# A decoder trunk: norms after the output projection, an own key buffer, attention levels issued together, outputs by ScalarE

## The chip, the cores and the metric

The kernel runs on one core of a Trainium2 chip. The metric is the device time of one execution in microseconds. The engines are named as in the profile: PE is TensorE (matrix products and transposes), PEld its loading of weights, DVE is VectorE, ACT is ScalarE, POOL is GpSimd, and SP issues the transfers. Each engine takes its instructions in the order in which they were placed in its queue, and waits on semaphores for results of others.

## What is computed

Two layers over 16 meta tokens and 2048 tokens of width 1024, all in fp32. The first is a gated convolution module, the second gated linear attention (GLA) with 4 heads, keys of 128 and values of 256. Each layer ends with `h = LayerNorm(alpha * h + mixer(h))`. Cut to what matters here:

```python
def conformer_mixer(h, ...):
    a, ga, z = split(h @ w_in + b_in, 3)
    c = causal_depthwise_conv31(a * sigmoid(ga)) + b_dw
    c = silu(layer_norm(c, norm_g, norm_b))
    return (c * silu(z)) @ w_out + b_out

def gla_mixer(h, ...):
    q, k, v, r, a1 = split(h @ w_in)
    g = log_sigmoid(a1 @ w_a2 + b_a) / 16
    # per chunk and head, b = cumsum(g) in the chunk:
    o = (q * exp(b)) @ S + att @ v,   att[t, s] = sum_d q[t,d] k[s,d] exp(b[t,d] - b[s,d]),  s <= t
    S = exp(b_last) * S + (k * exp(b_last - b)).T @ v
    o = o * rsqrt(mean(o * o) + eps) * norm_g
    return (o * silu(r)) @ w_out
```

## The kernel before, in words

Every large product is made three times: an fp32 operand is split into a high and a low part of a faster format (`split`, L72 to L74: ScalarE copies the high part, another engine subtracts), and `mm3` (L102 to L108) adds hi x hi, hi x lo and lo x hi into one PSUM tile. A scheduler orders the instructions of each engine when the program is built; the code's order is its input and buffer counts are its bounds. The order on TensorE is then fixed.

There are four stages. The first (to about 590 us) makes the convolution's inputs and taps, and isn't touched. The second (about 555 to 775 us) goes over 17 tiles of 128 tokens (`SUBS`; the last has 16): `norm(i)` (L311 to L337) loads the convolution's outputs into one of four buffers c, makes the mean by a small product (`mean`, L323), squares on ScalarE, adds up on GpSimd (`tree`), makes the variance by a small product (L330), a power on GpSimd, a diagonal dg (L334), a product `rb` (L335) that spreads the scale over the partitions, and multiplies c by it (L336). `gate(i)` (L345 to L357) does eight silus on ScalarE (L351), multiplies by silu(z) (L354), and splits the result into h_gt (ScalarE) and l_gt (VectorE). `out_proj(i)` (L418 to L425) makes the 48 products of 512 columns `y{i}`, adds the residual and does the layer norm. The loop (L427 to L435) runs norm, gate, projection; a head start before it has done three norms and one gate. A tile's y can't start before its h_gt.

The third stage (about 780 to 1550 us) is GLA: four blocks of 512 tokens (the first with the 16 meta tokens more) by four heads, so 16 units. `proj_units` issues the projections of the next head (k, q, v, r, and in `gates`, L626 to L643, the decay's cumulative sum b), and `gla_units` (L651 to L801) the work of the unit, in pieces that are interleaved by a debt counter in `phase3`. A unit does: kh = k exp(b_last - b) (L682 to L685: GpSimd, ScalarE, VectorE), its transposes pk (L693), the state products ds and the running state S (`state`), and the attention matrix of a 128-token chunk in levels m = 64, 32, 16, 8, 4, 2. For each level GpSimd (L719, L720), ScalarE and VectorE (L722, L723) make the decayed q and k, the tile A; levels 64 to 16 go into the PSUM tile att by products on sub-tiles of the array (L729), the rest into sm (L758, L760), which VectorE masks and reduces to red (32 by 32 blocks). at = red on the diagonal blocks plus att is split to a_h, a_l; the outputs o (L106 to L108) are squared on ScalarE with a sum (L783), copied (L784), scaled by the root mean square (L786 to L789), transposed (oT) and gated. The meta tokens' key buffer khm (L658) shares the tag kh and its one buffer with kh; kh's tile is also the place into which Square writes.

The last stage (about 1535 to 1727 us) is the output projection of GLA with its layer norm, and isn't touched.

Of the kernel before, what the change touches and what calls it, by code (L numbers as in the profile page):

```python
# [11 lines left out]
F32 = mybir.dt.float32  # L12
F32R = mybir.dt.float32r
AF = mybir.ActivationFunctionType
ALU = mybir.AluOpType
# [4 lines left out]
P = 128  # L20
# [15 lines left out]
RMS_EPS = 1e-6  # L36
# [13 lines left out]
class Trunk:  # L50
# [349 lines left out]
    def phase2(self, x_tok, wo, rows, h1_d, tail):  # L400
        nc = self.nc
# [10 lines left out]
        for i in range(3):  # L412
            t = const.tile([P, D], F32, name=f"row{i}")
# [14 lines left out]
        for i in range(ns):  # L428
            self.norm_next()
            self.gate_next()  # L430
            if self.nnorm == ns and not self.normed and self.st2:
                self.st2.close()
                self.st2 = None
                tail()
            out_proj(*self.gated.popleft())  # L435
        left.close()

# [19 lines left out]
    def phase3_init(self, wa2, pp, og_d):  # L457
        nc = self.nc
        self.og_d = og_d
        c0 = self.pool(self.st3, name="p3a", bufs=1)  # L460
# [4 lines left out]
        c = self.pool(self.st3, name="p3c", bufs=1)  # L465
        self.prm = c.tile([P, 8], F32, name="prm3")
        nc.sync.dma_start(self.prm[:, 0:6], pp)
        nc.vector.tensor_scalar(self.prm[:, 6:8], self.prm[:, 4:6], 0.5, None, op0=ALU.mult)

        raw = self.raw("a2")[:, :512]  # L470
# [155 lines left out]
    def gates(self, bi, h, hd, ns):  # L626
# [4 lines left out]
        for c0, m in ns:  # L631
            ps = self.pjt(f"z{bi}_{h}_{c0}")[:, :m]
            nc.tensor.matmul(ps, lhsT=self.wa2[:, h * P : (h + 1) * P], rhs=self.ah[:, c0 : c0 + m], start=True, stop=True)
            nc.vector.tensor_scalar(gl[:, c0 : c0 + m], ps, ba, 0.0, op0=ALU.add, op1=ALU.min)
            nc.scalar.activation(b[:, c0 : c0 + m], ps, AF.Abs, bias=ba)
        nc.scalar.activation(b[:, :n], b[:, :n], AF.Exp, scale=-1.0)
        nc.scalar.activation(b[:, :n], b[:, :n], AF.Ln, bias=1.0)
        nc.vector.tensor_tensor(gl[:, :n], gl[:, :n], b[:, :n], op=ALU.subtract)
        o = n - 512
# [11 lines left out]
    def gla_units(self, h, hd, bi, t0, n):  # L651
# [4 lines left out]
        if off:  # L656

            kh = self.gp.tile([P, 512], F32, tag="kh", name=f"khm{h}", bufs=1)[:, :off]  # L658
            nc.gpsimd.tensor_tensor(kh, b[:, off - 1 : off].to_broadcast([P, off]), b[:, :off], op=ALU.subtract)
# [32 lines left out]
        for c in range(4):  # L692
            nc.tensor.transpose(pt[:, c], kh4[:, c], K.ident)  # L693
        kth, ktl = self.pair3("k", pt, nc.vector, nm)
        Ss = []
# [17 lines left out]
        for m in (64, 32, 16, 8, 4, 2):  # L713
            A = self.gp.tile([P, 512], F32, tag="A", name=f"A{nm}_{m}", bufs=4)
            view = lambda x: x.rearrange("p (s u i) -> p s u i", u=2, i=m)
# [9 lines left out]
            if m >= 16:  # L725
                for c in range(4):
                    for s in range(0, P, 2 * m):
                        a = c * P + s
                        nc.tensor.matmul(  # L729
                            att[s : s + m, c, s + m : s + 2 * m],  # L730
                            lhsT=A[:, a : a + m],
                            rhs=A[:, a + m : a + 2 * m],
                            start=False,
                            stop=False,
                            skip_group_check=True,
                        )
                state(len(Ss))
                yield

# [10 lines left out]
        for c2 in range(2):  # L750
# [11 lines left out]
            nc.vector.tensor_tensor(ms, sm, K.lmask.unsqueeze(1).to_broadcast([P, 2, 144]), op=ALU.mult)  # L762
            rd = red[:, 2 * c2 : 2 * c2 + 2]
            nc.vector.tensor_reduce(rd, ms[:, :, 16:].rearrange("p c (l t) -> p c t l", t=32), axis=mybir.AxisListType.X, op=ALU.add)
            odd = rd.rearrange("p c (s u) -> p c s u", u=2)[:, :, :, 1]
            nc.vector.tensor_tensor(odd, odd, ms[:, :, :16], op=ALU.add)
            yield
        at = self.gp.tile([P, 4, 4, 32], F32, tag="at", name=f"at{nm}", bufs=1)
        for c in range(4):
            nc.vector.tensor_tensor(at[:, c], red[:, c].unsqueeze(1).to_broadcast([P, 4, 32]), K.blk, op=ALU.mult)  # L770
        nc.vector.tensor_tensor(at, at, att.rearrange("p c (a b) -> p c a b", b=32), op=ALU.add)
        ath, atl = self.pair3("a", at.rearrange("p c a b -> p c (a b)"), nc.gpsimd, nm, 1)
# [4 lines left out]
        junk = kh[:, :256]  # L777
        for c2 in range(2):
            o2 = self.pt.tile([P, 2, 256], F32, tag="g", name=f"o{nm}_{c2}")
            for c in (2 * c2, 2 * c2 + 1):  # L780
                o = o2[:, c % 2]
                self.mm3(o, [(qh[:, c], ql[:, c], *Ss[c]), (ath[:, c], atl[:, c], vh[:, c], vl[:, c])])
                nc.scalar.activation(junk, o, AF.Square, accum_out=sq[:, 0, c : c + 1])  # L783
            nc.vector.tensor_copy(osb[:, 2 * c2 : 2 * c2 + 2], o2)  # L784
            yield
        nc.vector.tensor_scalar(sq[:, 1], sq[:, 0], 1.0 / 256, RMS_EPS, op0=ALU.mult, op1=ALU.add)  # L786
        nc.gpsimd.tensor_tensor(sq[:, 2], sq[:, 1], self.mhalf, op=ALU.pow)
        for c in range(4):
            nc.vector.tensor_scalar(osb[:, c], osb[:, c], sq[:, 2, c : c + 1], None, op0=ALU.mult)  # L789
        yield  # L790
# [167 lines left out]
```

## Time and profile before

| | us |
|---|---|
| median of three runs (lowest, highest) | 1737.01 (1736.24, 1739.46) |
| the profiled execution | 1736.39 |
| its span in the trace | 1734.4 |
| PE busy in the span | 1679.1 (97%) |
| PEld busy | 1491.7 (86%) |
| DVE busy | 1396.5 (81%) |
| ACT busy | 841.4 (49%) |
| POOL busy | 938.4 (54%) |

The profile is that of one execution. Busy times are summed over instructions; a pipelined product counts as busy from its start to its modelled end, so what tells TensorE's rate is the distance of one start from the next. A wait is idle time of an engine, put down to the instruction that released it.

### The profile page before, as it was taken

What the parts mean: (1) busy time and instruction counts of PE and PEld (TensorE: products, weight loads), DVE (VectorE), ACT (ScalarE), POOL (GpSimd) and SP (SyncE); (2) the same over time, 40 slices, a digit from 0 to 9 for tenths busy, and PEclk for the clock granted to TensorE, in tenths of its full rate; (3) what the DMA queues carried; (4) which work ended last, traced back from release to release, by engine and by line L of the source; (5) the groups of instructions that cost most, each with busy time, mean ns of one, the idle gap of its engine ahead of it and who ended that gap; (6) DMA issues with size and microseconds to landing.
All of it is one profiled execution on the core that took longest, in us unless ns stands there. A gap on an engine that the chain in (4) does not pass through costs nothing.

```text
span 1734.4 us, 29031 instructions
## 1 busy us (share of the span) xinstructions
PE 1679.1 (97%) x11715; PEld 1491.7 (86%) x11715; DVE 1396.5 (81%) x1869; ACT 841.4 (49%) x1269; POOL 938.4 (54%) x675
## 2 busy tenths in 40 slices
PE   8999999999998998999999999999999999999998
PEld 8999999999998776778888888888888888788886
DVE  5789999999998898877776787777887788787665
ACT  6445555655544544445545454555555465541000
POOL 1879999999985788766332243332443153331000
PEclk9999999999999999999999999999999999999999
DMA  7110111111146644443122322223223322355441
GB/s 247 37 37 37 37 69 42 74 52 59 72 146 206 207 148 142 142 139 106 50 86 87 111 84 88 74 87 111 78 75 106 123 74 84 126 170 169 147 134 61
DMA packets 103910, 178.72 MB, mean 103 GB/s; under 512 B 8624, under 2 KB 68400, under 8 KB 103776
## 3 DMA queue, kind: packets, MB, share of 16 engines
q1 hardware_dynamic: 103776, 176.86, 30.4%
q8 instruction: 92, 1.51, 0.4%
q14 instruction: 42, 0.34, 0.1%
HBM read 134.70 MB, written 42.14 MB: 102 GB/s over the span
## 4 chain that ended last, share of the span: by engine, by line
PE 69%; DVE 12%; POOL 8%; ACT 5%; issue 3%; DMA 3%; SPq 0%; DVEq 0%; POOLq 0%; ACTq 0%
PE pj_y L106 4%; PE pj_y L108 4%; PE pj_y L107 4%; PE pj_g L107 3%; PE pj_g L108 3%; PE pj_g L106 3%; PE pj_z L107 3%; PE pj_z L106 3%; PE pj_a L107 3%; PE pj_a L106 3%; PE pj_z L108 3%; PE pj_a L108 3%; POOL A L720 1%; POOL A L719 1%; PE att L729 1%
## 5 line engine op out<-in xcount | busy, mean ns | idle before, releaser
L196 POOL TENSOR_TENSOR gacc<-gacc,prod 128x1024 f32<-128x1024 f32 (+1 forms) x156 | 385.9, 2477 | 63.1 <-ACT prod L195 54.2
L204 DVE SCALAR_TENSOR_TENSOR cacc<-glu,prm,cacc 128x1024 f32<-128x1024 f32 (+1 forms) x292 | 374.8, 1294 | 7.0
L195 ACT ACTIVATE prod<-glu,prm 128x1024 f32<-128x1024 f32 (+1 forms) x156 | 179.1, 1155 | 107.7 <-POOL gacc L196 107.3
L719 POOL TENSOR_TENSOR A<-b 128x256 f32<-128x256 f32 x96 | 80.2, 836 | 269.9 <-PE att L729 105.6
L106 PE MATMUL pj_g<-xh,h_w 128*128 128x412 f32 (+1 forms) x320 | 113.7, 355 | 5.6 <-ACT h_w L73 4.2
L107 PE MATMUL pj_g<-xl,h_w 128*128 128x412 f32 (+1 forms) x320 | 113.5, 355 | 0.3 <-DVE xl L74 0.3
L108 PE MATMUL pj_y<-woh,l_gt 128*128 128x512 f32 (+1 forms) x272 | 109.0, 406 | 4.3 <-DVE l_gt L74 4.2
L106 PE MATMUL pj_y<-woh,h_gt 128*128 128x512 f32 (+1 forms) x272 | 110.7, 410 | 1.9 <-ACT h_gt L73 1.8
L108 PE MATMUL pj_g<-xh,l_w 128*128 128x412 f32 (+1 forms) x320 | 112.5, 353 | 0.0
L107 PE MATMUL pj_z<-xl,h_w 128*128 128x412 f32 (+1 forms) x320 | 112.3, 351 | 0.0
L106 PE MATMUL pj_z<-xh,h_w 128*128 128x412 f32 (+1 forms) x320 | 112.2, 351 | 0.0
L107 PE MATMUL pj_a<-xl,h_w 128*128 128x412 f32 (+1 forms) x320 | 112.2, 351 | 0.0
L106 PE MATMUL pj_a<-xh,h_w 128*128 128x412 f32 (+1 forms) x320 | 112.1, 350 | 0.0
L108 PE MATMUL pj_z<-xh,l_w 128*128 128x412 f32 (+1 forms) x320 | 112.0, 351 | 0.0
L108 PE MATMUL pj_a<-xh,l_w 128*128 128x412 f32 (+1 forms) x320 | 111.9, 350 | 0.0
L107 PE MATMUL pj_y<-wol,h_gt 128*128 128x512 f32 (+1 forms) x272 | 110.6, 406 | 0.0
L106 PE MATMUL pj_y<-w4h,h_g 128*128 128x512 f32 x256 | 99.9, 391 | 0.0
L107 PE MATMUL pj_y<-w4l,h_g 128*128 128x512 f32 x256 | 99.8, 390 | 0.0
L108 PE MATMUL pj_y<-w4h,l_g 128*128 128x512 f32 x256 | 99.7, 389 | 0.0
L388 POOL TENSOR_TENSOR rs<-rs,mhalf 128x1 f32<-128x1 f32 x16 | 14.8, 923 | 155.7 <-DVE rs L387 155.7
L377 DVE SCALAR_TENSOR_TENSOR xt<-xt,pj_y 128x512 f32<-128x512 f32 (+1 forms) x66 | 44.5, 677 | 59.2 <-PE pj_y L108 59.2
L654 ACT ACTIVATE A<-A 128x512 f32<-128x512 f32 (+1 forms) x112 | 66.3, 597 | 46.0 <-POOL A L720 43.1
(428 smaller groups left out, 5264.0 us busy)
## 6 DMA issues: line engine op xcount, KB each, us to landing
r_w<-w SPq DMA_DIRECT2D x24, 512.0 KB, 3.2
c<-c_d SPq DMA_DIRECT2D x16, 512.0 KB, 4.5
szb<-sz_d SPq DMA_DIRECT2D x16, 512.0 KB, 4.6
xt<-x_tok SPq DMA_DIRECT2D x16, 512.0 KB, 4.5
h_d<-xt SPq DMA_DIRECT2D x16, 512.0 KB, 2.7
r_h1b<-h_d SPq DMA_DIRECT2D x16, 512.0 KB, 3.6
og_d<-og SPq DMA_DIRECT2D x32, 256.0 KB, 3.9
xt<-h_d SPq DMA_DIRECT2D x16, 512.0 KB, 3.5
```

Source lines behind the costliest of these rows:

```text
L106: mm(out, lhsT=lh, rhs=rh, start=(i == 0), stop=False)
L107: mm(out, lhsT=lh, rhs=rl, start=False, stop=False)
L108: mm(out, lhsT=ll, rhs=rh, start=False, stop=(i == n - 1))
L195: nc.scalar.activation(pr, src(k), AF.Copy, scale=tap(k))
L196: nc.gpsimd.tensor_tensor(st["g"], st["g"], pr, op=ALU.add)
L204: nc.vector.scalar_tensor_tensor(out, src(k), tap(k), acc, op0=ALU.mult, op1=ALU.add)
L377: self.nc.vector.scalar_tensor_tensor(xt[:m, es], xt[:m, es], ALPHA, ps, op0=ALU.mult, op1=ALU.add)
L388: nc.gpsimd.tensor_tensor(rs[:n, 2:3], rs[:n, 1:2], self.mhalf[:n, 0:1], op=ALU.pow)
L654: ex = lambda o, i: nc.scalar.activation(o, i, AF.Exp, scale=1.0 / TAU)
L719: nc.gpsimd.tensor_tensor(Av[:, :, 0], mid, bv[:, :, 0], op=ALU.subtract)
L720: nc.gpsimd.tensor_tensor(Av[:, :, 1], bv[:, :, 1], mid, op=ALU.subtract)
L729: nc.tensor.matmul(att[s : s + m, c, s + m : s + 2 * m], lhsT=A[:, a : a + m], rhs=A[:, a + m : a + 2 * m], start=False, stop=False, skip_ ...
```

## The change

1. The loop of the second stage calls `norm_next` after the projection instead of before the gate.
2. khm gets a buffer of its own; the pair of kh's transposes has one buffer instead of two.
3. The products of levels 64, 32 and 16 are issued together after level 16, chunk by chunk, those of 32 and 16 in one list; the state calls stay one for each level. The decay tile A has six buffers instead of four.
4. at begins as a copy of att by ScalarE; four VectorE additions on 32 rows then add red. Before, four products of red with a block mask and one addition did it on VectorE.
5. The outputs are scaled and copied out of PSUM by ScalarE, for two chunks at a time, after that half's own power; before, VectorE copied both halves and scaled them after one power for all four chunks.
6. In the gates min(z, 0) is made as Relu(-z) on ScalarE, and its sign is taken back in the following VectorE operation.

```diff
@@ phase2
         for i in range(ns):
-            self.norm_next()
             self.gate_next()
...
             out_proj(*self.gated.popleft())
+
+            self.norm_next()
@@ gates
-            nc.vector.tensor_scalar(gl[:, c0 : c0 + m], ps, ba, 0.0, op0=ALU.add, op1=ALU.min)
+            nc.scalar.activation(gl[:, c0 : c0 + m], ps, AF.Relu, bias=self.nba[:, h : h + 1], scale=-1.0)
...
-        nc.vector.tensor_tensor(gl[:, :n], gl[:, :n], b[:, :n], op=ALU.subtract)
+        nc.vector.scalar_tensor_tensor(gl[:, :n], gl[:, :n], -1.0, b[:, :n], op0=ALU.mult, op1=ALU.subtract)
@@ gla_units
-            kh = self.gp.tile([P, 512], F32, tag="kh", name=f"khm{h}", bufs=1)[:, :off]
+            kh = self.gp.tile([P, off], F32, tag="khm", name=f"khm{h}", bufs=1)
...
-        kth, ktl = self.pair3("k", pt, nc.vector, nm)
+        kth, ktl = self.pair3("k", pt, nc.vector, nm, 1)
...
-            A = self.gp.tile([P, 512], F32, tag="A", name=f"A{nm}_{m}", bufs=4)
+            A = self.gp.tile([P, 512], F32, tag="A", name=f"A{nm}_{m}", bufs=6)
...
             if m >= 16:
-                for c in range(4):
-                    for s in range(0, P, 2 * m):
+                state(len(Ss))
+                yield
+            if m == 16:
+
+                rest = ((32, 64), (16, 32), (16, 96), (32, 0), (16, 64), (16, 0))
+                for ms in (((64, 0),), rest):
+                    for c, (m, s) in ((c, x) for c in range(4) for x in ms):
                         a = c * P + s
                         nc.tensor.matmul(
                             att[s : s + m, c, s + m : s + 2 * m],
-                            lhsT=A[:, a : a + m],
-                            rhs=A[:, a + m : a + 2 * m],
+                            lhsT=lv[m][:, a : a + m],
+                            rhs=lv[m][:, a + m : a + 2 * m],
...
-                state(len(Ss))
-                yield
...
-        for c in range(4):
-            nc.vector.tensor_tensor(at[:, c], red[:, c].unsqueeze(1).to_broadcast([P, 4, 32]), K.blk, op=ALU.mult)
-        nc.vector.tensor_tensor(at, at, att.rearrange("p c (a b) -> p c a b", b=32), op=ALU.add)
+        nc.scalar.activation(at.rearrange("p c a b -> p (c a b)"), att.rearrange("p c t -> p (c t)"), AF.Copy)
+        for a in range(4):
+            rows = slice(32 * a, 32 * (a + 1))
+            nc.vector.tensor_tensor(at[rows, :, a], at[rows, :, a], red[rows], op=ALU.add)
...
-            nc.vector.tensor_copy(osb[:, 2 * c2 : 2 * c2 + 2], o2)
+            nc.vector.tensor_scalar(sq[:, 1, cs], sq[:, 0, cs], 1.0 / 256, RMS_EPS, op0=ALU.mult, op1=ALU.add)
+            nc.gpsimd.tensor_tensor(sq[:, 2, cs], sq[:, 1, cs], self.mhalf[:, cs], op=ALU.pow)
+            for c in (2 * c2, 2 * c2 + 1):
+                nc.scalar.activation(osb[:, c], o2[:, c % 2], AF.Copy, scale=sq[:, 2, c : c + 1])
             yield
-        nc.vector.tensor_scalar(sq[:, 1], sq[:, 0], 1.0 / 256, RMS_EPS, op0=ALU.mult, op1=ALU.add)
-        nc.gpsimd.tensor_tensor(sq[:, 2], sq[:, 1], self.mhalf, op=ALU.pow)
-        for c in range(4):
-            nc.vector.tensor_scalar(osb[:, c], osb[:, c], sq[:, 2, c : c + 1], None, op0=ALU.mult)
```

What the built programs' queues show of it stands below in three places: each line is one instruction with its line of code, operation, output, inputs and size; x4 means four alike in a row.

TensorE in the second stage, around the end of the products of tile 5 (y5) and the beginning of those of tile 6. Before:

```order
L108 MATMUL pj_y5_0_5201<-woh4_4619,l_gt5_5094 128x512
L335 MATMUL rb6_4969<-dg6_4974,mean_80 128x128
L330 MATMUL rb7_5073<-mean_80,sq7_5062 128x1
L106 MATMUL pj_y5_0_5201<-woh5_4625,h_gt5_5093 128x512
...
L108 MATMUL pj_y5_1_5227<-woh7_4637,l_gt5_5094 128x512
L335 MATMUL rb7_5073<-dg7_5078,mean_80 128x128
L330 MATMUL rb8_5175<-mean_80,sq8_5166 128x1
L106 MATMUL pj_y6_0_5305<-woh0_4595,h_gt6_5195 128x512
```

After:

```order
L106 MATMUL pj_y5_1_5207<-woh7_4637,h_gt5_5071 128x512
L107 MATMUL pj_y5_1_5207<-wol7_4638,h_gt5_5071 128x512
L108 MATMUL pj_y5_1_5207<-woh7_4637,l_gt5_5072 128x512
L335 MATMUL rb6_5051<-dg6_5056,mean_80 128x128
L323 MATMUL mean8_5250<-sq8_5248,mean_80 128x128
L330 MATMUL rb7_5155<-mean_80,sq7_5144 128x1
L106 MATMUL pj_y6_0_5283<-woh0_4595,h_gt6_5175 128x512
L107 MATMUL pj_y6_0_5283<-wol0_4596,h_gt6_5175 128x512
```

rb6 stood amid the products of tile 5, and now stands behind all of them, with two small products between it and the first product of tile 6. rb15 stands so before y15 as well.

GpSimd in the first GLA unit, from the meta tokens' khm on. Before:

```order
L659 TENSOR_TENSOR khm0_6811<-b0_0_6730 128x16
L719 TENSOR_TENSOR A0_0_64_6881<-b0_0_6730 128x4x64
L720 TENSOR_TENSOR A0_0_64_6881<-b0_0_6730 128x4x64
L719 TENSOR_TENSOR A0_0_32_6900<-b0_0_6730 128x8x32
...
L720 TENSOR_TENSOR A0_0_8_7013<-b0_0_6730 128x32x8
...
L683 TENSOR_TENSOR kh0_0_6827<-b0_0_6730 128x512
```

After:

```order
L662 TENSOR_TENSOR khm0_6813<-b0_0_6732 128x16
L686 TENSOR_TENSOR kh0_0_6829<-b0_0_6732 128x512
L722 TENSOR_TENSOR A0_0_64_6883<-b0_0_6732 128x4x64
L723 TENSOR_TENSOR A0_0_64_6883<-b0_0_6732 128x4x64
L722 TENSOR_TENSOR A0_0_32_6898<-b0_0_6732 128x8x32
L723 TENSOR_TENSOR A0_0_32_6898<-b0_0_6732 128x8x32
```

kh moved from behind four levels of A to the place right after khm.

TensorE in unit 2_1 (block 2, head 1), where level products (att), state products (ds) and projections (pj) take turns. Before, ahead of these rows the levels 64 and 32 stand apart, with one ds and projections between:

```order
L108 MATMUL pj_b2k2_0_12096<-xhb2_10540,l_b2k2_0_12013 128x512
L729 MATMUL att2_1_12045<-A2_1_16_12122 16x16 x6
L106 MATMUL ds2_1_1_12084<-vhb2v1_11813,k_h2_1_12007 128x256
L107 MATMUL ds2_1_1_12084<-vlb2v1_11814,k_h2_1_12007 128x256
L108 MATMUL ds2_1_1_12084<-vhb2v1_11813,k_l2_1_12008 128x256
L729 MATMUL att2_1_12045<-A2_1_16_12122 16x16 x10
L758 MATMUL sm2_1_0_12186<-A2_1_8_12153 32x32 x4
```

After, all levels of the unit:

```order
L108 MATMUL pj_b2k2_0_12086<-xhb2_10542,l_b2k2_0_12015 128x512
L737 MATMUL att2_1_12047<-A2_1_64_12049 64x64
L106 MATMUL ds2_1_0_12059<-vhb2v1_11818,k_h2_1_12009 128x256
L107 MATMUL ds2_1_0_12059<-vlb2v1_11819,k_h2_1_12009 128x256
L737 MATMUL att2_1_12047<-A2_1_64_12049 64x64 x3
L108 MATMUL ds2_1_0_12059<-vhb2v1_11818,k_l2_1_12010 128x256
L737 MATMUL att2_1_12047<-A2_1_32_12064 32x32
L737 MATMUL att2_1_12047<-A2_1_16_12112 16x16 x2
L737 MATMUL att2_1_12047<-A2_1_32_12064 32x32
```

The levels stand in one piece now, with three state products among them, and no projection in between.

## Rows read from the trace of the kernel before

**Rows 1.** The page's busy table: us, share of the span, instructions.

```profile
PE 1679.1 (97%) x11715; PEld 1491.7 (86%) x11715; DVE 1396.5 (81%) x1869; ACT 841.4 (49%) x1269; POOL 938.4 (54%) x675
```

**Rows 2.** Busy us by stretch: PE, PEld, DVE, ACT, POOL; then granted clock, DMA.

```profile
600.00:660.00 60.00, 57.77 (x258) 46.22 (x257) 55.18 (x68) 26.99 (x46) 52.79 (x39) 1.00 0.50 163
660.00:700.00 40.00, 31.91 (x131) 24.08 (x130) 32.59 (x40) 18.39 (x32) 35.20 (x29) 0.93 0.48 150
...
1250.00:1350.00 100.00, 98.94 (x926) 85.92 (x926) 79.36 (x138) 53.83 (x97) 36.03 (x38) 1.00 0.28 91
```

**Rows 3.** PE's waits, 560 to 780 us: us in total, times, longest.

```profile
PE pj_y L108 <- DVE l_gt L74: 4.2, 4, 2.5
...
PE rb L335 <- DVE dg L334: 0.2, 1, 0.2
```

**Rows 4.** PE's waits, 780 to 1560 us: first, third, fifth and last.

```profile
PE pk L693 <- DVE kh L685: 5.2, 3, 3.9
...
PE o L106 <- ACT a_h L73: 4.0, 3, 2.5
...
PE o L108 <- POOL a_l L74: 2.8, 4, 0.8
...
PE trb L495 <- issue: 0.2, 1, 0.2
```

**Rows 5.** Timeline of PE, first GLA unit: start, duration, idle before in brackets.

```profile
830.12 1.12 PE L693 MATMUL pk<-ident,kh 128*128 128x128 f32 x4 [3.86 <-DVE kh L685]
...
832.01 0.42 PE L107 MATMUL pj_b0k<-xlb,h_b0k 128*128 128x264 f32 x1
832.23 0.42 PE L108 MATMUL pj_b0k<-xhb,l_b0k 128*128 128x264 f32 x1
```

**Rows 6.** Busy time from 830 to 835 us, columns as in rows 2.

```profile
830.00:835.00 5.00, 4.88 (x30) 4.49 (x31) 4.62 (x10) 2.17 (x4) 1.37 (x2) 0.54 0.58 204
```

**Rows 7.** Timeline of GpSimd, the same unit.

```profile
824.61 1.22 POOL L683 TENSOR_TENSOR kh<-b 128x512 f32<-128x512 f32 x1
```

**Rows 8.** Timeline of PE: tile shapes change at 1123.27 and at 1125.05.

```profile
1122.71 0.39 PE L107 MATMUL pj_b1r<-xlb,h_b1r 128*128 128x512 f32 x1
1122.94 0.40 PE L108 MATMUL pj_b1r<-xhb,l_b1r 128*128 128x512 f32 x1
1123.27 0.68 PE L729 MATMUL att<-A 128*64 128x64 f32 x8
...
1125.05 0.50 PE L106 MATMUL pj_b1k<-xhb,h_b1k 128*128 128x512 f32 x1
1125.38 0.39 PE L107 MATMUL pj_b1k<-xlb,h_b1k 128*128 128x512 f32 x1
```

**Rows 9.** Timelines of PE, DVE and ACT: one tile's way from rb to h_gt.

```profile
627.12 0.38 PE L335 MATMUL rb<-dg,mean 128*128 128x128 f32 x2
...
627.54 1.22 DVE L336 TENSOR_TENSOR c<-c,rb 128x1024 f32<-128x1024 f32 x1 [0.35 <-PE rb L335]
...
628.79 3.19 ACT L351 ACTIVATE c<-c,prm 128x128 f32<-128x128 f32 x8 [0.51 <-DVE c L336]
...
632.43 1.44 DVE L354 TENSOR_TENSOR c<-c,szb 128x1024 f32<-128x1024 f32 x1
...
633.90 1.06 ACT L73 ACTIVATE h_gt<-c 128x1024 fp32r<-128x1024 f32 x1 [1.92 <-DVE c L354]
```

**Rows 10.** Groups of instructions, 780 to 1560 us: busy us, mean ns (L604: min/median/max ns).

```profile
L783 ACT ACTIVATE kh<-o 128x256 f32<-128x256 f32 x60 | 22.9, 382 | 55.0 <-PE o L108 54.4
L784 DVE COPY osb<-o 128x512 f32<-128x512 f32 x30 | 20.5, 685 | 16.3 <-ACT kh L783 16.3
L789 DVE TENSOR_SCALAR osb<-osb,sq 128x256 f32<-128x256 f32 x60 | 19.9, 394 | 1.2 <-POOL sq L787 1.2
...
L770 DVE TENSOR_TENSOR at<-red,blk 128x128 f32<-128x128 f32 x60 | 16.5, 311 | 0.3
...
L604 DVE TENSOR_TENSOR ah<-at,ah x17: 156/283/284, 794.1 to 1384.8; 32x128 fp32r<-32x128 f32 x16, 32x16 fp32r<-32x16 f32 x1
```

More of the change, by code (lines that the diff above doesn't have):

```diff
@@ L468, in phase3_init @@
         nc.vector.tensor_scalar(self.prm[:, 6:8], self.prm[:, 4:6], 0.5, None, op0=ALU.mult)
+        self.nba = c.tile([P, 4], F32, name="nba3")
+        nc.vector.tensor_scalar(self.nba, self.prm[:, 0:4], -1.0, None, op0=ALU.mult)
         raw = self.raw("a2")[:, :512]
@@ L778, in gla_units @@
         for c2 in range(2):
+            cs = slice(2 * c2, 2 * c2 + 2)
             o2 = self.pt.tile([P, 2, 256], F32, tag="g", name=f"o{nm}_{c2}")
```

## Prediction

> **What bounds the kernel now.** I read the busy table first: TensorE is busy for 97% of the span [rows 1], so only time that TensorE loses counts; work taken off another engine is worth nothing unless TensorE waits for that engine. Second came the table by stretches. In the output projection of the convolution (600 to 700 us) VectorE and GpSimd are nearly as full as TensorE, 55.2 and 52.8 of 60 us, and from 660 to 700 TensorE works only 31.9 of 40 us at a granted clock of 0.93; in the attention stage (1250 to 1350) VectorE has 79% and ScalarE 54%, and TensorE 98.9% [rows 2]. Third came TensorE's waits in the two stages that the change touches. Between 560 and 780 us there are seven kinds that sum to 14.4 us (first and last of them in [rows 3]); between 780 and 1560 us thirteen kinds that sum to 26.1 us (four of them in [rows 4]). More than 40 us is therefore not to be had from waits. The first stage (up to about 590 us) and the last keep their order of work on TensorE, and I count them at zero.
>
> **The key buffer.** The largest wait of the attention stage is 3.86 us before the key transposes pk of the first unit, and it ends with VectorE's kh [rows 5]. GpSimd starts kh only at 824.61, behind all decays of the unit, because khm holds the one buffer [rows 7]. After the change kh stands directly behind khm. Then the transposes find kh long done, and the wait goes whole: 3.9 us. It is followed by half clock: from 830 to 835 us the granted clock was 0.54, close to the lower level of 1.2 GHz, with TensorE busy 4.88 us [rows 6]; the 264-column products start every 0.22 us there [rows 5], where the 0.23 us of 512 columns [rows 8] give 0.12. Lost work: 0.46 x 4.88 = 2.2 us. What TensorE did before the fall was to stand idle for those 3.86 us. Without the idle time both go, **-6.1 us**. The decays start one GpSimd step of 1.22 us later [rows 7]; nothing is late next, since their products on TensorE now wait for the third level anyway and have the head's projections ahead of them. The other two waits of pk (5.2 - 3.9 us [rows 4]) I count as gone too, since kh in later units stands no later in GpSimd's order: **-1.3**.
>
> **Products of three levels together.** Where TensorE goes from 128-row products to 64- or 32-row tiles and back, the next start comes 0.33 us after the last instead of 0.23, both ways [rows 8]: 0.10 us per change of tile shape. In the built program's order of TensorE I count 265 such changes before and 217 after; the products themselves are the same in number and shape. 48 x 0.10 = **-4.8 us**. Six decay buffers only allow this; they cost no instruction. The bound from the other side: if the pause belongs to something else than the shape, nothing is gained here.
>
> **ScalarE's outputs, the attention sum and the gates.** Per unit VectorE loses two copies and four scalings, 2 x 0.685 + 4 x 0.394 = 2.9 us, and four products with the block mask, 4 x 0.311 = 1.2 us [rows 10]; four additions on 32 rows of the same length replace these four (taken at 1.1 to 1.2 us, since a subtraction on 32 rows of 128 elements takes 0.283 us now, at the median [rows 10]). One full-size addition goes as well. The gates trade two VectorE operations for one. ScalarE gets four copies of 256 columns from PSUM; nearest is its Square of the same tile, 0.382 us [rows 10], so 1.5 us, and about 1.3 us more for the copy of att and the Relu. So roughly 4 us a unit leave VectorE and 3 us come to ScalarE: over a unit's 48 us VectorE falls from 79% to about 71%, ScalarE rises from 54% to about 60%. Neither bounds, so this moves waits only. The products o wait for ScalarE's a_h 4.0 us and for GpSimd's a_l 2.8 us [rows 4]; both lie behind the sum att that VectorE makes. The copy on ScalarE can run before the reductions, and the queue on VectorE is shorter; but the copy and a_h now queue on a fuller ScalarE. I take half: **-3.4** (bounds 0 and -6.8). Against it stand new small waits: the outputs' PSUM tile is now held through Square, a scale, GpSimd's power and two copies, and the power runs twice a unit. For 16 units I allow 0.25 us each, **+4** (bounds 0, and +16 at 1 us each, which is one wait of the size that a_h has now).
>
> The Trainium skill speaks against this part: "Trainium Architecture — The Big Picture", section "The five engines, in one table", says that ScalarE is not for simple arithmetic, VectorE being up to about three times faster per element. By that the four copies would take up to 4.7 us a unit, and each half's transposes could come 1.6 us later, 16 x 1.6 = 26 us if TensorE came to wait for every unit, about 1752 us in all. The trace doesn't bear it out: ScalarE's 256 columns take 0.382 us with a square and VectorE's 0.394 [rows 10], so I give it a chance of 0.02, within the slower cases.
>
> **Late norms.** In the second stage a tile's norm ends on TensorE with the small product rb; from there the way to the next products y is serial: VectorE's product with rb (starts 627.54), eight silus on ScalarE (628.79, 3.19 us), the product with silu(z) (632.43), ScalarE's split (633.90, 1.06 us): from 627.12 to 634.96, 7.8 us [rows 9]. In the order before, tiles 6 and 15 have rb 31 and 48 products ahead of their y, at 0.23 us each, so most of the 7.8 us is hidden. After the change rb of tile 6 and of tile 15 stand at the end of the previous tile's products, with y6 and y15 right behind (0.6 us of other work at tile 6; at tile 15 rb of tile 16 and twelve transposes, about 1.6 us, but also the silus of tile 16 ahead of the split, some 2.4 us, an estimate below the 3.19 of [rows 9]). Other tiles keep 39 products (9.0 us) and more. TensorE takes its queue in order, so it must stand for about 7.2 us at tile 6 and 7.6 at tile 15: +14.8 us, each followed by half clock as in [rows 6], 2 x 2.2 = 4.4 us. I leave 3 us for other tiles. Together 22.2 us. It replaces the 14.4 us of waits there now [rows 3], nearly all of them waits for these norms' steps, and the slow clock of 660 to 700 us, (1 - 0.93) x 40 = 2.8 us [rows 2]. Net **+5.0 us**; bounds: -8 if only one of the two stalls comes, with its clock (9.4 against 17.2), and +24 with the first rival below.
>
> **Sum.** -6.1 - 1.3 - 4.8 - 3.4 + 4 + 5.0 = -6.6 us. The profiled run of 1736.4 us (its span 1734.4 us and 2.0 around it) lies 0.6 below the median of 1737.0, so the same difference gives 1730.4 us, about **1730**.
>
> **Rivals.** (1) Slower: the late norms cost far more. The place is the 7.8 us way behind rb; VectorE and GpSimd run at 92% and 88% there [rows 2], so its two VectorE steps and the split can queue behind the post-norm of the tile before. It decides once the way takes longer than the 9.0 us that the other tiles have: at 11 us each of some eight tiles loses 2 us and the two bare stalls 3 us more each, 22 us less the 3 us left for them above, 1730 + 19 = about 1749. For it: the chain shown has idle steps already (it takes 7.8 us for 7.2 us of work). Against: the late norms are what keeps VectorE's queue free just then. (2) The same time: TensorE's waits of the attention stage are not cured but handed on to ScalarE, which now carries Square, scales, the att copy and a_h; new waits of 0.65 us a unit instead of 0.25 cost 6.4 us more, 1736.4. (3) Much faster: with VectorE relieved all of a_h and a_l goes (-3.4 more), no new waits come (-4), and a third of the two stalls (5 us) is covered: about 1718. (4) The grouping does less than its name: the three state products still stand among the levels, as in unit 2_1; if a change costs nothing where the next weights are loaded early, the 4.8 us don't come: about 1735, within the bound.
>
> **Chances.** A measurement of this kernel tells about 0.2% from no change, 1733.5 to 1740.5. Forecast 0.46, rival 3 0.16, rivals 2 and 4 together 0.20, rival 1 with the mechanism of slow copies 0.18. The forecast's own range is 1724 to 1737, so 0.04 of it lies within the bound, and 0.02 of rivals 2 and 4 ends faster. Faster 0.60, same 0.22, slower 0.18. The range for 8 in 10 goes from 1717 (rival 3) to 1746 (most of rival 1 but its far end).
>
> **What would show it.** Right: no wait of TensorE before pk of the first unit and a granted clock of 1.00 there; two waits of 6 to 9 us at y6 and y15, for ScalarE's h_gt, with a lower clock behind each; the sum of waits of o for a_h and a_l below 4 us; about 0.1 us less at each place where levels were apart. Wrong: stalls at most tiles of the second stage (rival 1), waits of oT for osb or of o for Square above 8 us in all (rival 2), or y6 and y15 without a wait (rival 3). The prediction fails most easily on the net of the second stage, where two numbers of 17 and 22 us are subtracted.

## The result and the profile after

The changed kernel takes 1766.33 us (median of four runs, 1764.09 to 1768.54) where the kernel before took 1736.62, measured beside it: 1.0159 times as long, 95% interval 1.0142 to 1.0175. The forecast was 1730, with a range to 1746. The profiled run took 1766.63 us, its span is 1764.9, which is 30.5 us more.

First the busy table of the changed kernel, to be read against [rows 1], and its busy time by stretch (PE, PEld, DVE, ACT, POOL, then granted clock), against [rows 2]:

```profile
PE 1682.0 (95%) x11715; PEld 1498.8 (85%) x11715; DVE 1372.5 (78%) x1754; ACT 879.7 (50%) x1369; POOL 941.0 (53%) x691
```

```profile
600.00:660.00 60.00, 50.15 (x208) 40.41 (x207) 48.29 (x55) 23.27 (x37) 48.08 (x35) 0.89 0.45 143
660.00:700.00 40.00, 38.27 (x175) 30.86 (x173) 34.88 (x44) 18.22 (x32) 30.63 (x26) 1.00 0.49 147
1250.00:1350.00 100.00, 93.66 (x877) 80.40 (x872) 71.97 (x118) 55.32 (x100) 34.45 (x38) 0.98 0.24 81
```

The work moved as meant: VectorE has 24 us less and ScalarE 38 us more, and TensorE has the same products. But TensorE is idle more: in the stretch 1250 to 1350 it works 93.7 us instead of 98.9, while VectorE has 7.4 us less to do (the changed kernel is some 25 us behind there, so the work isn't quite the same). Only ScalarE is a little fuller than before (55.3 against 53.8), and still all of it is slower. Where the time went is seen from the start of the same products in both traces:

| first product of | before, us | after, us | later by |
|---|---|---|---|
| tile 5 of the second stage | 621.5 | 624.8 | 3.3 |
| tile 6 | 636.9 | 646.5 | 9.6 |
| block 0, first head's v, which follows tile 16 | 783.3 | 799.2 | 15.9 |
| block 0, second head's v | 849.5 | 861.6 | 12.1 |
| block 3, last head's v | 1512.1 | 1540.9 | 28.8 |
| the last stage | 1544.4 | 1577.9 | 33.5 |
| end of the span | 1734.4 | 1764.9 | 30.5 |

The second stage loses about 16 us, by the second head's v the attention stage has won 4 back, and from there to its end it loses more than 16, a little at a time.

TensorE's waits of the changed kernel in the two stages (us in total, times, longest). Second stage, whole list, to [rows 3]:

```profile
PE pj_y L106 <- ACT h_gt L73: 9.0, 3, 8.1
PE trb L498 <- DMA r_h1b<-h_d: 4.2, 1, 4.2
PE mean L323 <- DVE sq L321: 3.9, 1, 3.9
PE trb L498 <- DVE c L336: 2.8, 1, 2.8
PE rb L330 <- POOL sq L343: 1.8, 1, 1.8
PE rb L335 <- DVE dg L334: 1.7, 1, 1.7
PE mean L323 <- POOL sq L343: 1.1, 1, 1.1
```

Attention stage, the largest three and two others, to [rows 4]:

```profile
PE o L106 <- ACT kh L792: 10.3, 13, 1.7
PE o L106 <- ACT a_h L73: 6.7, 3, 3.6
PE o L106 <- DVE xlb L501: 5.9, 3, 3.5
...
PE oT L802 <- ACT osb L796: 1.8, 1, 1.8
...
PE o L108 <- POOL a_l L74: 0.5, 1, 0.5
```

In the first list the sum is 24.5 us instead of 14.4, and two places make most of it: y6, and the end of the stage. In the second the whole list sums to 41.7 us instead of 26.1. The wait for kh before pk, the largest before, is gone, and the outputs o now wait thirteen times for ScalarE's Square (kh is only where Square writes its junk; in the code the chunk that is squared and the one that the product makes are the two halves of one PSUM tile, o2). One such place, on ScalarE's and then TensorE's timeline (start, duration, idle before):

```profile
1123.09 0.63 ACT L657 ACTIVATE A<-A 128x512 f32<-128x512 f32 x1 [0.42 <-POOL A L723]
1124.71 0.63 ACT L657 ACTIVATE A<-A 128x512 f32<-128x512 f32 x1 [0.99 <-POOL A L723]
1125.25 0.36 ACT L792 ACTIVATE kh<-o 128x256 f32<-128x256 f32 x1
1125.51 0.19 ACT L792 ACTIVATION_READ_ACCUMULATOR kh<-o 128x1 f32 x1
1126.22 0.63 ACT L657 ACTIVATE A<-A 128x512 f32<-128x512 f32 x1 [0.51 <-POOL A L723]
1126.76 0.36 ACT L792 ACTIVATE kh<-o 128x256 f32<-128x256 f32 x1
...
1127.27 0.38 PE L106 MATMUL o<-sh,q_h 128*128 128x256 f32 x1 [1.74 <-ACT kh L792]
```

ScalarE isn't full here. It stands idle before the exponentials of the next unit's decays A, each of which waits for GpSimd, and the Square that TensorE waits for is queued behind them: the products that it squares had all started by 1121.45. In the built programs' order, and in the traces, four exponentials of the next unit's levels stand ahead of this unit's last Square in most units before the change, six after. That is what six decay buffers did, and the experiments test it.

### The profile page after: what moved, and what is told of

The parts are those of the page before. It is cut to its first block, busy times and chain, and to the rows that moved or that the text cites. A ratio compares the mean times of both kernels' runs of the same rounds, so it can differ in the third digit from the quotient of the medians.

```text
span 1764.9 us, 29000 instructions
## 1 busy us (share of the span) xinstructions
PE 1682.0 (95%) x11715; PEld 1498.8 (85%) x11715; DVE 1372.5 (78%) x1754; ACT 879.7 (50%) x1369; POOL 941.0 (53%) x691
## 4 chain that ended last, share of the span: by engine, by line
PE 67%; DVE 14%; ACT 6%; POOL 6%; issue 4%; DMA 3%; SPq 0%; DVEq 0%; POOLq 0%; ACTq 0%
PE pj_y L108 5%; PE pj_y L107 5%; PE pj_y L106 5%; PE pj_g L107 3%; PE pj_g L106 3%; PE pj_g L108 3%; PE pj_z L107 3%; PE pj_z L106 3%; PE pj_a L106 3%; PE pj_a L107 3%; PE pj_z L108 3%; PE pj_a L108 3%; DVE A L726 2%; DVE A L725 2%; POOL A L723 1%
## 5 line engine op out<-in xcount | busy, mean ns | idle before, releaser
L74 POOL TENSOR_TENSOR a_l<-at,a_h 128x512 fp32r<-128x512 f32 x16 | 22.2, 1387 | 180.4 <-issue 153.4
```

What stands on the lines that cost most here:

```text
L74: eng.tensor_tensor(lo, raw, hi, op=ALU.subtract)
```

## Experiments

Ratios are to the kernel before, measured beside each run, with 95% intervals; a time without a ratio is that run's median. Two runs that were not measured side by side are best compared by their ratios.

**The late norms undone, and alone.** In the changed kernel `norm_next()` goes back ahead of the gate; then the kernel before gets the late norms only:

```diff
         for i in range(ns):
-            self.norm_next()
             self.gate_next()
...
             out_proj(*self.gated.popleft())
+            self.norm_next()
```

> The changed kernel with one part undone: norm_next stands ahead of the gate again, everything else stays. Theory (the late norms cost what the second stage shows, 14 us of lost TensorE time more than before): 1766 - 14 = 1752 us, no wait of 8 us before y6. Rival (part of the delay is given back later, since the third stage is held by VectorE, GpSimd and ScalarE and not by TensorE): 1758 to 1764 us.

> The kernel before with the late norms alone. Theory (bare stalls at y6 and at the end of the second stage, 12 to 14 us as between the changed kernel and the one with early norms): 1748 to 1752 us. Rival (the cost came from the third stage's new beginning and not from the norms): 1736 to 1742 us.

Undone: 1754.3 us, 1.0083 (1.0054 to 1.0112), so 12.0 less than the changed kernel (13 by the ratios). Alone: 1754.1 us, 1.0086 (1.0058 to 1.0113), about 15 us more than before, and nothing of it is given back: in that run's trace the delay of 19 us at the end of the second stage is still 18 us at the start of the last. The theory holds, with 12 to 13 us where 14 was expected and 15 where it was 12 to 14; the rivals fall.

**Late norms with a longer head start** (and khm's own buffer). The head start makes four norms instead of three:

```diff
-            for _ in range(CB - 1):
+            for _ in range(CB):
                 t.norm_next()
```

> khm's own buffer, late norms, and a head start of four norms instead of three, so that the norms' lead over the projections is what it was: rb stands 48 products ahead of its y in every tile, none at 0. Theory (the late norms cost by the lost lead alone, through rb directly ahead of y6 and y15): the waits at y6 and y15 are gone, 1733 to 1737 us. Rival (making a norm after the projection costs in itself, by VectorE and GpSimd busy with the post-norm then): 1745 to 1752 us.

1739.3 us, 1.0008 (0.9997 to 1.0019), against 1735.5 for khm's own buffer with the norms early, and a little above the 1733 to 1737 that the theory gave. The built order has every rb 48 products ahead of its y again, none at 0, and the waits of y for h_gt are gone. In their place stands, largest of that run:

```profile
PE rb L335 <- DVE dg L334: 11.1, 6, 2.7
```

So of the 15 us some 11 are the lost lead; the rest, about 4 us between runs that were not measured side by side, is near what can be told.

**Six, five and three decay buffers.** Six in the kernel before, with one buffer for the pair of kh's transposes to make room; five so, on top of khm's own buffer; three on top of khm's own buffer; and the control, the single pair on top of khm's own buffer:

```diff
-        kth, ktl = self.pair3("k", pt, nc.vector, nm)
+        kth, ktl = self.pair3("k", pt, nc.vector, nm, 1)
...
-            A = self.gp.tile([P, 512], F32, tag="A", name=f"A{nm}_{m}", bufs=4)
+            A = self.gp.tile([P, 512], F32, tag="A", name=f"A{nm}_{m}", bufs=6)
```

> The kernel before with six decay buffers A instead of four (and one buffer for the pair of kh's transposes, which makes the room); products of the levels, outputs and norms as before. Theory (six buffers let all six decays of the next unit stand ahead of the last Square of this unit on ScalarE, so the products o wait): 1746 to 1753 us, waits of o for Square above 8 us in all. Rivals (the ScalarE outputs do it, or the grouped levels do it): 1735 to 1739 us, waits of o for Square as before, 3.6 us.

> khm's own buffer with five decay buffers (one buffer for the pair of kh's transposes makes the room). Three buffers gave 1738, four 1735.5, and the kernel before with six 1759 us. If the cost goes with the number of exponentials ahead of the last Square (five here): 1743 to 1750 us. If it comes only with the sixth (the whole next burst ahead): 1735 to 1739 us.

> khm's own buffer with three decay buffers instead of four. The theory of the burst is that each buffer lets one more decay of the next unit stand ahead of this unit's tail: three exponentials instead of four ahead of the last Square. If only that counts, the waits of o and oT shrink and it takes 1728 to 1735 us. Rival (with three buffers GpSimd waits for the products of the levels, and the decays themselves come late for att and sm): 1740 to 1755 us.

> khm's own buffer and one buffer instead of two for the pair of kh's transposes; four decay buffers. It is the control of the runs with five and six buffers, which had this edit too. If the decay buffers alone are the cause: 1734 to 1738 us. If the single pair is what costs: 1745 us and more.

Six: 1758.8 us, 1.0109 (1.0079 to 1.0139). Five: 1758.1, 1.0117 (1.0095 to 1.0138). Three: 1738.3, 1.0007 (0.9995 to 1.0018). The single pair: 1736.0, 0.9985 (0.9972 to 0.9997), as khm's buffer without it. So the fifth and sixth buffers cost about 20 us (19 from the kernel before, 22 from khm's own buffer), more than expected, and the pair nothing. The cost doesn't go with the number of exponentials, as I had thought: it comes whole with the fifth buffer, and three are no better than four. What the buffers bound is seen on GpSimd, in the row of the decays' first subtraction from 780 to 1560 us, with four (the kernel before), then with six:

```profile
L719 POOL TENSOR_TENSOR A<-b 128x256 f32<-128x256 f32 x96 | 80.2, 836 | 269.9 <-PE att L729 105.6 <-DVE b L643 104.1 <-PE pj_b2q L107 25.8
L719 POOL TENSOR_TENSOR A<-b 128x256 f32<-128x256 f32 x96 | 80.2, 836 | 230.1 <-DVE b L643 120.2 <-PE pj_b2q L108 40.9 <-PE pj_b3q L108 20.8
```

With four, GpSimd's decays wait 105.6 us for products att that free a buffer; with six that wait isn't among the named. The named wait on TensorE was wrong: with VectorE making the outputs, the waits of o for Square are 2.0 us, and the largest is that of the outputs' transposes, with one row of its timeline and two of VectorE's below it (six buffers):

```profile
PE oT L794 <- DVE osb L789: 13.2, 5, 4.7
PE o L108 <- POOL a_l L74: 6.7, 6, 2.3
...
1227.14 1.16 PE L794 MATMUL oT<-ident,osb 128*128 128x128 f32 x4 [4.74 <-DVE osb L789]
...
1212.05 0.65 DVE L786 TENSOR_SCALAR sq<-sq 128x4 f32<-128x4 f32 x1
...
1226.75 1.13 DVE L789 TENSOR_SCALAR osb<-osb,sq 128x256 f32<-128x256 f32 x4
```

From the mean square (L786) to the scaling (L789) VectorE's queue takes 14.7 us, with the twelve decay multiplications of the next unit's levels in it. The same place with four buffers and khm's own buffer:

```profile
1205.74 0.28 DVE L786 TENSOR_SCALAR sq<-sq 128x4 f32<-128x4 f32 x1
...
1211.72 1.26 DVE L722 TENSOR_TENSOR A<-A,b2k 128x256 f32<-128x256 f32 x1
1212.90 0.41 DVE L723 TENSOR_TENSOR A<-A,b2q 128x256 f32<-128x256 f32 x1
...
1214.66 2.16 DVE L789 TENSOR_SCALAR osb<-osb,sq 128x256 f32<-128x256 f32 x4
```

There it is 8.9 us with eight. The last three of these take 0.41 us, the others 0.83 and more. Two of the 16 units look like this; in the others the next unit's multiplications stand ahead of the mean square too, and mostly 1.3 to 3.5 us lie between the two rows. Counted in the traces, with the one of A1 (L745), 9 multiplications of the next unit stand ahead of this unit's scaling in nearly all units with four buffers, 11 with five, 13 with six and 7 with three. So what is shown is the mechanism in its general form (more of the next unit's decays stand in the queues ahead of this unit's tail), and not the particular wait; which of the tail's steps is last depends on who makes the outputs. Why the step from 9 to 11 costs the whole 20 us, and those from 7 to 9 and from 11 to 13 next to nothing, stays open.

**Levels together or apart.** The changed kernel with early norms and the levels issued apart (the loop over c and s of the kernel before), with six and with four buffers; and together with four buffers, VectorE's outputs and khm's own buffer:

> The changed kernel with early norms and with each level's products issued after its own level again; six buffers, ScalarE outputs and khm's own buffer stay. It is to be read against the changed kernel with early norms, 1754.3 us. If grouping gains what the prediction said by fewer changes of tile shape: 1759 us. If six buffers with ScalarE outputs lose as their single runs say (20 + 8.5 - 6) and grouping is what took a part back: 1759 to 1765 us. If grouping itself costs: below 1752 us.

> As the run before it (early norms, levels apart, ScalarE outputs, khm's own buffer), with four decay buffers instead of six. Theory (the burst of six decays costs in this setting too): 15 to 20 us below the run with six, 1740 to 1745 us. Rival (with ScalarE's outputs the burst harms less, since VectorE's queue no longer holds the outputs): within 6 us of the run with six.

> As the run before it, with the three levels' products issued together and four decay buffers. Grouping took 4 us off where there were six buffers. With four, the products of all three levels wait for level 16, so eight of the next unit's decay multiplications stand ahead of this unit's at on VectorE in ten units (in two before). If that queue on VectorE costs as the six buffers do: 1745 to 1755 us. If the fewer changes of tile shape are what counts: 1731 to 1735 us.

Apart, six: 1758.3 us, 1.0110. Apart, four: 1742.2, 1.0022 (1.0010 to 1.0033). Together, four: 1765.4, 1.0155 (1.0124 to 1.0187). Six buffers cost 16 us with ScalarE's outputs too. Grouping takes 4.0 us off where there are six (1758.3 to 1754.3; two runs each, 2.7 to 5.4 between single ones), and adds some 29 us where there are four and VectorE makes the outputs (against 1736.0; neither answer expected that much). Its three largest waits there:

```profile
PE o L106 <- ACT a_h L73: 9.3, 10, 1.9
PE ds L106 <- DVE Sm L707: 6.0, 5, 1.5
PE sm L761 <- DVE og L799: 4.6, 3, 2.5
```

Ten waits for a_h: this time it is at that stands behind eight multiplications of the next unit, as the built order had shown.

**khm's own buffer alone.**

```diff
-            kh = self.gp.tile([P, 512], F32, tag="kh", name=f"khm{h}", bufs=1)[:, :off]
+            kh = self.gp.tile([P, off], F32, tag="khm", name=f"khm{h}", bufs=1)
```

> The kernel before with one edit: khm in a buffer of its own. The prediction's step: no wait of 3.9 us before the first pk and no half clock behind it, 1736.6 - 6.1 = 1730.5 us. Rival (the decays and GpSimd's queue behind kh are late instead, and the gain is given back within the unit): 1735 to 1738 us.

1735.5 us, 0.9987 (0.9976 to 0.9998): 2.3 us, not 6.1. The wait of 3.86 us [rows 5] is gone, but two rows of that place in the new trace (a timeline row of TensorE, and the stretches 825 to 835 us) show what came next:

```profile
826.81 0.69 PE L667 MATMUL dsm<-vm,ktm 16*128 16x256 f32 x2 [1.17 <-ACT ktm L665]
```

```profile
825.00:830.00 5.00, 3.83 (x38) 2.94 (x37) 5.00 (x9) 3.72 (x8) 3.43 (x4) 0.89 0.02 3
830.00:835.00 5.00, 5.00 (x60) 4.66 (x59) 4.58 (x9) 2.21 (x5) 2.27 (x3) 0.77 0.65 209
```

The meta tokens' small product waits 1.17 us, and half clock comes all the same, for less time (0.89 and 0.77, where it was 0.54 [rows 6]), now behind an idle time of a little over 1 us. Two of the later waits of pk, 1.4 us in all, stand as before.

**The ScalarE part**: all of it from the kernel before; the changed kernel with VectorE's outputs again; then, on top of khm's own buffer, each of its three pieces alone.

> The kernel before with the ScalarE part alone: Relu in the gates, the copy of att, the outputs scaled and copied by ScalarE after each half's power; four decay buffers, levels apart, norms early, khm in the shared buffer. Theory (six buffers are the cause): 1728 to 1737 us. Rival (the output tile in PSUM is held longer and ScalarE is fuller, and this makes the waits of o): 1746 to 1753 us with waits of o for Square above 8 us.

> The changed kernel with the outputs copied and scaled by VectorE again after one power for all four chunks; all else stays (late norms, six buffers, grouped levels, att copy and Relu on ScalarE). Theory (six buffers): 1762 to 1769 us, waits of o for Square still above 8 us. Rival (ScalarE outputs): 1750 to 1756 us, those waits back at about 4 us.

> khm's own buffer (1735.5 us) with the outputs scaled and copied by ScalarE after each half's own power, nothing else. It splits the ScalarE part, which costs about 6 us between khm alone and khm with all of it. Theory (the outputs now wait for a power on GpSimd and two copies in ScalarE's queue before oT, and this is the part that costs): 1739 to 1743 us with waits of oT for osb above 2 us. Rival (another part costs): 1731 to 1736 us.

> khm's own buffer with the copy of att by ScalarE and four additions on 32 rows, nothing else. Theory (outputs cost): 1732 to 1736 us. Rival (a_h comes later, since four additions that queue with the next unit's decays stand behind the copy): 1739 to 1743 us with waits of o for a_h and a_l above 9 us (7.5 with khm alone).

> khm's own buffer with Relu on ScalarE in the gates, nothing else. Theory (outputs cost): 1734 to 1737 us, since 16 operations of 0.7 us change engines off TensorE's way. Rival: 1739 us and more, with b later in each unit and so the whole burst of decays later.

All of it: 1748.0 us, 1.0056 (1.0034 to 1.0078), 9 us more than before; with khm's own buffer and the single pair it was 1742.2 above, about 6 us over khm alone. The pieces, against 1735.5: outputs 1736.6 (0.9992, 0.9981 to 1.0003), at 1741.9 (1.0020), gates 1740.5 (1.0019). So the outputs, which I had suspected, cost next to nothing, and at and the gates some 5 us each; their sum is above the 6 us that all of it cost over khm alone. The time of at is the rival's, but not its waits: a_h and a_l fell to 3.8 us in all. In the changed kernel VectorE's outputs make it 20 us slower, 1786.5: with six buffers ScalarE is the better place for them. The waits of at alone, and of the gates alone:

```profile
PE o L106 <- ACT kh L784: 8.5, 11, 1.4
PE o L106 <- DVE xlb L498: 5.6, 3, 2.7
...
PE o L108 <- POOL a_l L74: 0.5, 1, 0.5
```

```profile
PE o L108 <- POOL a_l L74: 8.9, 8, 2.7
PE oT L796 <- DVE osb L791: 5.6, 2, 2.8
```

With khm alone these were 3.7 (Square), 1.8 (xlb), 3.7 (a_l) and 0.9 (osb). Each piece does shorten a wait (a_l from 3.7 to 0.5 with at), and another grows by more. Why by more was not settled; each edit makes the scheduler place the whole unit anew, so a difference of 5 us says little of a mechanism. The 16 to 22 us of the buffers, found in three settings, stand well above that.

## Why the prediction was wrong

**The decay buffers: the step that failed.** "Six decay buffers only allow this; they cost no instruction." They cost 16 us (apart, four to six) to 20 us (alone). I had looked for what the edit adds to the engines, found nothing, and not asked what it lets the scheduler bring forward. The four buffers were a bound: the fifth decay had to wait until the products of the first level had read theirs, and until then the tail of the unit before got through VectorE, GpSimd and ScalarE. The danger could have been read blind, from the count of exponentials ahead of the last Square, four and six, in the built orders; its price could not, since five cost as much as six. The allowance of 4 us for new waits had an upper end of 16, about what the buffers cost, but I had put it to the output tile in PSUM, which the outputs' own run shows to be innocent with four buffers. My second rival had its sign: o waits 10.3 us for Square, above its 8, and 7.2 us for a_h and a_l where I wanted less than 4. Two things raise the wait for Square: the buffers (4.2 us with four, 8.5 with six, levels apart) and the copy of att on ScalarE (8.5 alone). The rival had the second and not the first, and its 6.4 us are far from the 36 us that the forecast missed.

**Levels together.** The term held in size, 4.0 against 4.8 us, in a kernel with six buffers. That the fewer changes of shape are the whole of it isn't shown: in the traces of the two runs with six buffers the changes to or from the sub-tiles of att and sm fall from 190 to 160, 3 us at 0.10 each, and the granted clock differs as well (0.989 and 0.988 apart, 0.990 and 0.992 together). Nor does the pause need a change of shape: behind transposes of full shape the next start also takes 0.32 us (782.07 to 782.39 in the changed kernel). That the grouping loses 29 us with four buffers I did not see; four buffers with ScalarE's outputs were not run, but in the runs made its gain doesn't come without the buffers' price.

**Late norms.** The place and the size of the bare stall at y6 were right: 7.2 us forecast, 8.1 found. The way from rb to h_gt, and the first product behind it at half clock (0.43 us apart):

```profile
637.67 0.39 PE L335 MATMUL rb<-dg,mean 128*128 128x128 f32 x2
...
638.82 1.21 DVE L336 TENSOR_TENSOR c<-c,rb 128x1024 f32<-128x1024 f32 x1
...
640.07 3.19 ACT L351 ACTIVATE c<-c,prm 128x128 f32<-128x128 f32 x8 [3.02 <-DVE c L336]
...
645.39 1.06 ACT L73 ACTIVATE h_gt<-c 128x1024 fp32r<-128x1024 f32 x1 [1.19 <-DVE c L354]
...
646.50 0.79 PE L106 MATMUL pj_y<-woh,h_gt 128*128 128x512 f32 x1 [8.10 <-ACT h_gt L73]
647.09 0.63 PE L107 MATMUL pj_y<-wol,h_gt 128*128 128x512 f32 x1
647.52 0.63 PE L106 MATMUL pj_y<-woh,h_gt 128*128 128x512 f32 x1
```

At the end of the stage TensorE stands 2.8 and 4.2 us before transposes of the next stage that are queued ahead of y15, 7.0 us in all where 7.6 was forecast, though under other names; y15 itself then waits 0.2 us for h_gt, so it could not have begun sooner:

```profile
773.09 0.79 PE L106 MATMUL pj_y<-woh,h_gt 128*128 128x512 f32 x1 [0.21 <-ACT h_gt L73]
```

The 7.6 agrees in part by luck: the prediction's own terms, 7.8 - 1.6 + 2.4, give 8.6, and the other work between rb and y15 took 2.9 us instead of 1.6. Two terms were mis-sized. One is the "3 us for other tiles": the means, variances and diagonals still wait 8.5 us (3.9, 1.8, 1.7 and 1.1 in the list above). I had let all 14.4 us of the waits before go, and most of the norms' share stayed. The other is the clock, 4.4 us for two falls less the 2.8 of before. The changed kernel has four stretches at half clock there instead of two, one of them behind an idle time of 1.75 us (624 to 629 us, below, with the columns of [rows 2]) and one amid the other tiles:

```profile
624.00:629.00 5.00, 4.40 (x13) 3.53 (x14) 4.67 (x7) 1.50 (x3) 2.36 (x3) 0.66 0.89 250
645.00:650.00 5.00, 3.50 (x10) 2.91 (x11) 4.46 (x7) 1.06 (x1) 5.00 (x6) 0.50 0.56 178
700.00:705.00 5.00, 3.92 (x13) 3.09 (x12) 4.56 (x7) 3.18 (x6) 4.72 (x5) 0.53 0.89 271
770.00:775.00 5.00, 3.03 (x9) 2.06 (x10) 4.46 (x10) 5.00 (x11) 0.55 (x1) 0.50 0.24 91
```

By the prediction's way of counting, (1 - granted clock) x busy over 5 us stretches from 575 to 800 us, that is 9.6 us, and 2.7 before. Net 12 to 15 instead of 5.0. My first rival had the right sign and stage, 19 us over the forecast; its mechanism, eight tiles that each lose 2 us, did not come: the other tiles' y wait 0.9 us.

**The key buffer.** 2.3 us instead of 6.1. The wait went, but "nothing is late next" was wrong, and the clock, which I had tied to the wait of 3.86 us, fell as well behind a shorter one. The other two waits of pk, counted as gone for 1.3 us, stand as they were. In the changed kernel the clock is 1.00 there, and no wait of pk is left.

**ScalarE's part.** The sum of its two terms, -3.4 and +4, was near zero; it is about +6. The factor that the Trainium skill gives as the most ("Trainium Architecture — The Big Picture", "The five engines, in one table": VectorE up to about three times faster) was not reached here: the four copies take 0.471 us each on ScalarE, where VectorE's scalings took 0.394 and its copies out of PSUM 0.685 for twice the columns [rows 10], so 1.2 to 1.4 times.

```profile
L796 ACT ACTIVATE osb<-o,sq 128x256 f32<-128x256 f32 x62 | 25.9, 471 | 29.6 <-POOL sq L794 29.6
```

**The sum as the runs have it**: khm -2.3 (0.9987), ScalarE's part about +6, decay buffers +16, grouping -4, late norms +12: 28 us, where the changed kernel was measured 29.7 over the kernel before. These are the steps of one chain of runs from the kernel before to the changed one, so that they come out near the whole is no evidence; what bears them out is the same edits elsewhere, the buffers at 19 and 22 us and the late norms at 15. ScalarE's part (9 in the kernel before) and the grouping (29 with four buffers) have no price apart from their surroundings. Forecast were -6.1 - 1.3, +0.6, 0, -4.8 and +5.0. Of all the kernels, only khm's own buffer alone (and with the single pair) is faster than the kernel before, by 0.1% to 0.2%.

## What to carry to other kernels

Where a scheduler fills in-order queues, a buffer count is an order: one buffer more can let the next unit's work stand ahead of the present unit's tail, and cost 20 us in 1737 with no engine busier. So count, in the built order, what of the next unit stands ahead of each result that the bounding engine waits for, before and after, on the engines that make it. The count gives a warning and not a price: here two buffers more cost 16 to 20 us, the fifth as much as both, and one buffer less gained nothing. And when a stall is priced, the waits that it is to replace have to be taken off one by one, not as a sum.

## What the hardware showed that was not expected

With khm's own buffer TensorE fell to half clock (0.89 and 0.77 over two stretches of 5 us) behind a stretch in which it was idle for only 1.17 us of 5. In the changed kernel it stayed at 1.00 through a stretch with an idle time of 2.03 us (845 to 850 us, 2.79 of 5 busy), so the length of the idle time alone doesn't tell. VectorE's 256-column multiplication of two SBUF tiles took 0.83 us beside GpSimd's subtractions and copies and 0.41 us beside its power on 4 columns (1212.90 to 1213.99 us with khm's own buffer); the Trainium skill's page "SBUF — State Buffer" (section "SBUF: two separate sides") says that the two share a port pair that one holds for a whole instruction, and the doubling agrees with it.
